# Moving sums of a pooling branch at earlier weight pieces, and two chunks of its products side by side through ScalarE and VectorE

## The chip, the cores and the metric

The kernel runs on one core of a Trainium2 chip. The time is device microseconds (us) of that core for one launch of the whole program: from the inputs in device memory to the output there. The engines of the core are named as the profile names them: PE is TensorE (PEld its weight loads), DVE is VectorE, ACT is ScalarE, POOL is GpSimd, and SP is SyncE, which issues most of the DMA transfers.

## The reference

A trunk of two layers works on 256 tokens of 1024 channels, in float32. Each layer has a token mixer and a gated MLP with a short convolution. The change lies in the mixer's pooling branch. Its part of the reference, with what stands around it (dilated attention, gates and the MLP are left out):

```
D_MODEL, SEQ, DEPTH = 1024, 256, 2
POOL_WINDOWS = (2, 4, 8, 16)
...
def _centred_mean(u, window):
    c = jnp.pad(jnp.cumsum(u.astype(jnp.float32), axis=1), ((0, 0), (1, 0), (0, 0)))
    i = np.arange(S)
    lo = np.clip(i - window // 2, 0, S)
    hi = np.clip(i - window // 2 + window, 0, S)
    count = (hi - lo).astype(np.float32)
    return ((c[:, hi] - c[:, lo]) / count[None, :, None]).astype(u.dtype)
...
def _token_mixer(xn, w_in, w_pool, pool_scale, w_a, w_b, w_o, rel_bias):
    u, q, k, v, g_pool, g_attn = jnp.split(xn @ w_in, SPLITS, axis=-1)
    ug = u.reshape(B, S, POOL_GROUPS, POOL_GROUP_DIM)
    pooled = jnp.stack([_centred_mean(ug[:, :, gi], w) for gi, w in enumerate(POOL_WINDOWS)], axis=2) - ug
    pool_out = jnp.einsum('bsgc,gcd->bsgd', pooled, w_pool).reshape(B, S, POOL_WIDTH) * pool_scale
    ...
    merged = jax.nn.sigmoid(g_pool) * (pool_out @ w_a) + jax.nn.sigmoid(g_attn) * (attn_out @ w_b)
    return merged @ w_o
```

So four groups of 256 channels are each averaged over a centred window of 2, 4, 8 or 16 tokens, the token itself is taken away, each group is multiplied with its own 256 x 256 matrix and scaled per channel, and the result (8 chunks of 128 channels) goes into the product with w_a.

## The kernel before, in words

**Products in two parts.** Every float32 operand of a large product is split into a high part in a reduced format and the rest (a low part), and three products are made: high by high, high by low, low by high. A weight reaches the core as `raw` by DMA from SyncE's queue, ScalarE casts it to the high part `wh` (L214) and VectorE subtracts to get the low part `wl` (L216). The class `Weights` does this in the order of use. A *piece* is 128 x 1024 elements; a load brings two pieces; three raw buffers and five pairs of `wh`, `wl` turn. `W.get()` hands out the next piece, and first writes the splits up to four pieces further on into the program; so a split stands in ScalarE's and VectorE's queues where the piece some four ahead of it is taken. A raw buffer is free for the next load when the low part of its second piece is made.

**Where the branch lies.** In each layer the values come first, then the 1024 channels of u (8 pieces), then query and key rows of the attention: six blocks `n` of 4 pieces each (`by_tokens`, L702, tile `t_ps`). Behind each of these pieces stands a *place*, 0 to 23 for these blocks, and the table `steps` says what is written into the program at which place. From here to the gates the three engines PE, ACT and DVE run in order of the source (`manual_schedule`): an engine never takes a later instruction ahead of one that waits. After a block, its rows are transposed by VectorE (`cross`, L749, tile `qk_rows`), written to device memory by SyncE (`crossing`) and read back by GpSimd's queue.

**The moving sums.** `pool_window(gi)` is a generator for window 2, 4, 8, 16 (`gi` 0 to 3). ScalarE copies u into a padded tile (L1013); VectorE doubles the window by one addition after the other (L1022: one addition for window 2, four for window 16), mends the edges (L1031, L1035), and makes the centred input `pd` (L1037); ScalarE casts its high part (L1045) and VectorE makes its low part `pl` (L1046). It yields after each addition, after `pd`, and after `pl`: 3 + 4 + 5 + 6 = 18 parts for the four windows. `pool(n)` in `steps` runs the next n parts. Before, two parts stand at places 4 to 6, one at 7, two at each of 8 to 12, and one at 13.

**The branch's products.** `pool_out` runs beside block n = 3, whose four pieces are numbered 33, 34, 36 and 37 in layer 0; two more pieces, 32 and 35, hold the four groups' matrices. Ahead of each of the four pieces, one group's products are made (`two_sums`, L578, tile `pool_ps`): two chunks `oc` of 128 channels, eight matmuls each. `pool_ps` takes a buffer of a PSUM pool of four. A chunk then goes through four operations that alternate between two engines: ScalarE multiplies the second half-sum by the scale (L1070), VectorE multiplies the first and adds (L1071, tile `po`; this frees the PSUM buffer), ScalarE casts the high part (L1074), VectorE makes the low part (L1075). The `po` tile turns in three buffers. All four operations of a chunk are written before those of the next.

In the instruction orders below, the numbers behind a tile's name are the program's own; for weights, `wh37` and `wl37` are the two parts of piece 37.

Of the kernel before, what the change touches and what calls it, by code (L numbers as in the profile page):

```python
# [10 lines left out]
F32 = mybir.dt.float32  # L11
F32R = mybir.dt.float32r
AF = mybir.ActivationFunctionType
ALU = mybir.AluOpType
# [240 lines left out]
def encoder(ctx, tc, x, w_in, w_pool, pool_scale, w_a, w_b, w_o, norm1, norm2, w_up, conv_w,  # L255
            conv_b, w_down, rel_bias, norm_f, onehot, edges, out):
    nc = tc.nc
# [43 lines left out]
    for l in range(DEPTH):  # L301
# [11 lines left out]
        for n, pairs in enumerate(BLOCKS):  # L313
            for base in (C_Q, C_K):
                pool = ([], [])
                if n == 1 and base == C_K:
                    pool = W.add(
                        w_pool[l].rearrange("g (k p) c -> p (g k) c", p=P), (8, 256),
                        [((lambda t, j=j: t[:, 4 * j : 4 * j + 4, :]), (4, 256)) for j in range(2)],
                    )  # L320
                    pool = (pool[:1], pool[1:])
# [18 lines left out]
        for kind, n in PLAN:  # L340
            if kind in "AG":
                j = halves_done.get((kind, n), 0)
# [65 lines left out]
    hps = const.tile([P, DEPTH, 8], F32, name="hps")  # L408
# [156 lines left out]
    def two_sums(x2, nk, *chunks):  # L565

        wide, rests = ([(c, k, kind) for c in chunks for k in range(nk)] for kind in (True, False))
        first = rests if turns["rest"] else wide
        last = wide if turns["rest"] else rests
        for steps in (first, last):
            for (ps, wh, wl), k, kind in steps:
                out, w, x = (ps, wh, x2[:, k]) if kind else (ps[:, 1], wl, x2[:, k, 0])
                nc.tensor.matmul(  # L578
                    out, w(k), x, start=(steps is first and k == 0),
                    stop=(steps is last and k == nk - 1), skip_group_check=turns["rest"],  # L580
                )
        turns["rest"] = not turns["rest"]
# [21 lines left out]
    def halves(a):  # L604

        return a.rearrange("p (t m) -> p t m", t=2)
# [86 lines left out]
    def v_tile():  # L693
        return acc.tile([P, 512], F32, tag="acc", name="v_ps")
# [12 lines left out]
    def by_tokens(x2, n, at_once=1, then=None, ps=None, begin=0, end=None,  # L707
                  ahead=None):


        if ps is None:
            ps = [mmp.tile([P, 512], F32, tag="mm", name="t_ps") for _ in range(2)]
        for i0 in range(begin, n if end is None else end, at_once):
            if ahead:
                next(ahead)
            held = [W.get() for _ in range(at_once)]
            for t in range(2):
                for i, piece in enumerate(held, i0):
                    v_sum(ps[t], x2, t, i, piece, n - 1)
            for i, _ in held:  # L720
                W.free(i)
            if then:
                then()
        return ps

    def to_chunks(rows, y, z, parts):

        turned = nc.vector.transpose(out=y.rearrange("p q c j -> p c q j"), in_=rows)  # L730
        d = dram.tile([P, 4, P], F32, tag="turned", bufs=4, name="turned")
        nc.sync.dma_start(out=d, in_=y.rearrange("p q c j -> p q (c j)"))
        for q in range(4):
            there = nc.sync.dma_start(
                out=z[32 * q : 32 * q + 32].rearrange("p a c j -> p a (c j)"),
                in_=d[:, q].rearrange("(a i) x -> i a x", a=4),
            )
        hi, lo = (p.rearrange("p c (a j) -> p a c j", a=4) for p in parts)
        made = nc.scalar.copy(out=hi, in_=z), nc.vector.tensor_sub(out=lo, in0=z, in1=hi.bitcast(F32))
        return turned, there, made  # L740
# [23 lines left out]
    def two_parts(tag, name):  # L764


        return big.tile([P, KD, 2, 2, P], F32R, tag=tag, name=name)
# [174 lines left out]
    for l in range(DEPTH):  # L942
# [25 lines left out]
        else:  # L968
            for g in range(NG):
                held = begun[0] if g == 0 else [W.get() for _ in range(4)]  # L970
                for t in range(2):
                    if g + t == 0:
                        ps = begun[1]
                    else:
                        ps = v_tile()
# [22 lines left out]
        for n in range(2):  # L998
            ps = by_tokens(x2, 4)
# [56 lines left out]
        def pool_out(po2):  # L1056
            for j in range(2):
                i, (wh, wl) = W.get()
                for gg in range(2):
                    for oc in range(2):  # L1060
                        ps = acc.tile([P, 2, S], F32, tag="acc", name="pool_ps")
                        cc = slice(oc * P, (oc + 1) * P)
                        two_sums(
                            pooled[2 * j + gg], 2,
                            (ps, lambda k: wh[:, 2 * gg + k, cc], lambda k: wl[:, 2 * gg + k, cc]),
                        )
                        c = 4 * j + 2 * gg + oc
                        sc = hps[:, l, c : c + 1]
                        po = sm.tile([P, 2, P], F32, tag="p", bufs=3, name="po")
                        nc.scalar.mul(out=po, in_=halves(ps[:, 1]), mul=sc)  # L1070
                        nc.vector.scalar_tensor_tensor(  # L1071
                            out=po, in0=halves(ps[:, 0]), scalar=sc, in1=po, op0=ALU.mult, op1=ALU.add
                        )
                        nc.scalar.copy(out=po2[:, c, 0], in_=po)  # L1074
                        nc.vector.tensor_sub(out=po2[:, c, 1], in0=po, in1=po2[:, c, 0].bitcast(F32))  # L1075
                    if gg:
                        W.free(i)
                    yield
# [103 lines left out]
        def keep_pa(n):  # L1182
# [7 lines left out]

            **{n: ((pool, 2),) for n in (4, 5, 6)},
            7: ((pool, 1),),
            **{n: ((pool, 2),) for n in range(8, 13)},
            13: ((pool, 1),),
            16: ((parts, 0),),
            17: ((parts, 1),),
            19: ((bring, 0),),
# [25 lines left out]
        po2 = None  # L1223
        for n in range(6):
            block, which = divmod(n, 2)
            if n == 3:
                po2 = two_parts("m2", "po2")
            ps = by_tokens(x2, 4, then=step, ahead=pool_out(po2) if n == 3 else None)
            y = rows_of_tmp(1)
            if n in (2, 4):  # L1230
                z = tmp[:, 0].rearrange("p (a c j) -> p a c j", a=8, c=4)
            else:

                z = zu[:, 0] if n == 1 else kk[:, (1, None, None, 0, None, 1)[n]]
            cross(ps, y, z, "crossing")
            if n == 3:

                highs = big.tile([P, 2, HPG, 2, P], F32R, tag="xn", name="highs")
                qh, kh = highs[:, 0], highs[:, 1]
                lows = [  # L1240
                    big.tile([P, 2, 2, 2, P], F32R, tag=f"{tag}0", name="lows") for tag in "qk"
                ]
                turned_p = big.tile([P, 2, 2 * 4, 4, 32], F32, tag="ybig", name="turned_p")
# [15 lines left out]
        for n in range(2):  # L1259
            th = gate("q1")  # L1260
            for t in range(2):
                nc.vector.scalar_tensor_tensor(
                    out=pa[n][:, t], in0=th[:, t], scalar=1.0, in1=pa[n][:, t],
                    op0=ALU.add, op1=ALU.mult,
# [4 lines left out]
        made = None  # L1269
        turned_rows = big.tile([P, 2, 2, 4, 4, 32], F32, tag="xn", name="turned")  # L1270
        for n, cc in enumerate(HALVES):
# [6 lines left out]
            ps = by_tokens(at2, 2, 2)  # L1278
# [3 lines left out]
            for t in range(2):  # L1282

                with tc.issue_after((turning if t else made[1]).ins) if n + t else ExitStack():
                    nc.vector.scalar_tensor_tensor(
                        out=th[:, t], in0=th[:, t], scalar=1.0, in1=ps[t], op0=ALU.add, op1=ALU.mult
                    )
                    nc.vector.tensor_add(out=th[:, t], in0=th[:, t], in1=pa[n][:, t])
                turning, there, made = to_chunks(
                    th[:, t], y[:, t], z[:, t], (mh[:, ks, t], ml[:, ks, t])  # L1290
                )
# [179 lines left out]
```

## Time and profile before

| | |
|---|---|
| median of 3 runs | 862.19 us |
| the runs | 860.63, 862.19, 864.61 us |
| the profiled execution | 862.41 us, of which the profile's span is 860.6 us |
| mean granted TensorE clock | 0.996 |
| PE busy | 848.0 us (99%) |
| DVE, ACT busy | 664.5 us (77%), 489.5 us (57%) |
| pool_ps matmuls | 32 + 32, from 95.5 to 535.0 us (two layers) |

The span runs from the first to the last instruction; the execution's own time is some 2 us longer. Rows of the timeline read: start in us, length in us, engine, source line, operation, output <- inputs, shape, count, and in brackets how long the engine stood idle just before and what released it. Rows of a count over one merge equal instructions, and their length runs from the first start to the last end. Matmuls overlap in these rows, so the pace of PE is read from start to start. Rows of the windows view give for each engine the busy time and the count in that stretch, then the granted TensorE clock, the busy share of the DMA engines and GB/s. SPq and POOLq are the queues that issue DMA.

### The profile page before, as it was taken

The page shows a single profiled execution, that of the slowest core. Times are in us where ns is not written, and L with a number is a line of the kernel's source. Part 1 is how long each engine was busy: PE and PEld are TensorE (multiplying, and loading weights), DVE is VectorE, ACT ScalarE, POOL GpSimd, SP SyncE. Part 2 cuts the span into 40 slices and gives each one's busy share as a digit, 9 for nine tenths or more (in the row PEclk, how much of TensorE's full clock was granted, in tenths as well). Part 3 has the DMA queues.
Part 4 walks back from the last instruction along what each step waited for, and adds up shares of the span by engine and source line. Part 5 has one row for each costly group of instructions (what it writes and reads, how often), then busy time and mean ns, then how long its engine had stood idle before and what let it go on. Part 6 is the DMA issues. An engine that isn't in the chain of part 4 may idle for free.

```text
span 860.6 us, 11236 instructions
## 1 busy us (share of the span) xinstructions
PE 848.0 (99%) x3959; PEld 708.6 (82%) x3959; DVE 664.5 (77%) x994; ACT 489.5 (57%) x759; POOL 133.3 (15%) x274
## 2 busy tenths in 40 slices
PE   9999999999999999999999999999999999999996
PEld 7888878888888888888888887888888888888885
DVE  7957887877767869889855598787676778797894
ACT  7735473655545556667645355655454555666682
POOL 1811212120011221220000212132100122121201
PEclk9999999999999999999999999999999999999999
DMA  9689878994749888976627888788857498798831
GB/s 332 210 245 337 245 244 289 296 310 165 252 176 295 263 274 265 291 264 212 240 98 237 264 257 260 243 274 300 267 187 278 136 304 268 248 294 287 254 143 49
DMA packets 117697, 211.95 MB, mean 246 GB/s; under 512 B 7864, under 2 KB 45440, under 8 KB 117640
## 3 DMA queue, kind: packets, MB, share of 16 engines
q1 hardware_dynamic: 109032, 187.89, 65.5%
q0 software_dynamic: 8448, 23.08, 10.1%
q8 instruction: 31, 0.51, 0.2%
q10 hardware_dynamic: 160, 0.27, 0.1%
q14 instruction: 26, 0.21, 0.1%
HBM read 184.97 MB, written 26.23 MB: 245 GB/s over the span
## 4 chain that ended last, share of the span: by engine, by line
PE 84%; DVE 9%; DMA 3%; issue 1%; ACT 1%; SPq 1%; POOLq 0%; DVEq 0%; POOL 0%; ACTq 0%
PE t_ps L702 51%; PE v_ps L702 6%; PE res_ps L620 6%; PE res_ps L622 5%; PE res_ps L621 5%; DVE wl L216 4%; DMA raw<-in_w_in_dram 3%; PE v_ps L934 3%; PE proj_ps L578 2%; PE v_ps L841 1%; DVE us L1022 1%; PE o_ps L1151 1%; PE s_ps L1098 1%; DVE qk_rows L749 1%; PE s_ps L1092 1%
## 5 line engine op out<-in xcount | busy, mean ns | idle before, releaser
L702 PE MATMUL t_ps<-wh,x 128*128 128x512 f32 x1344 | 421.2, 390 | 0.0
L216 DVE TENSOR_TENSOR wl<-raw,wh 128x1024 fp32r<-128x1024 f32 x274 | 331.0, 1217 | 104.7 <-ACT wh L214 102.0
L214 ACT CAST wh<-raw 128x1024 fp32r<-128x1024 f32 x274 | 285.7, 1050 | 172.9 <-PE t_ps L702 117.0
L702 PEld LDWEIGHTS t_ps<-wh,x 128*128 128x128 f32 x1344 | 252.7, 188 | 52.7
L702 PE MATMUL t_ps<-wl,x 128*128 128x512 f32 x672 | 261.7, 389 | 0.0
L702 PEld LDWEIGHTS t_ps<-wl,x 128*128 128x128 f32 x672 | 126.4, 188 | 25.9
L620 PE MATMUL res_ps<-wh,actq 128*128 128x512 f32 (+1 forms) x184 | 70.2, 381 | 0.1
L621 PE MATMUL res_ps<-wl,actq 128*128 128x512 f32 (+1 forms) x184 | 69.9, 380 | 0.0
L622 PE MATMUL res_ps<-wh,actk 128*128 128x512 f32 (+1 forms) x184 | 69.8, 380 | 0.0
L702 PE MATMUL t_ps<-wh,po 128*128 128x512 f32 x128 | 40.8, 393 | 0.0
L620 PEld LDWEIGHTS res_ps<-wh,actq 128*128 128x128 f32 x184 | 34.6, 188 | 7.5 <-ACT actq L1405 1.0
L622 PEld LDWEIGHTS res_ps<-wh,actk 128*128 128x128 f32 x184 | 34.6, 188 | 6.9 <-DVE actk L1406 0.4
L621 PEld LDWEIGHTS res_ps<-wl,actq 128*128 128x128 f32 x184 | 34.6, 188 | 6.5
L756 POOL DMA_DIRECT2D zga<-crossing x32 | 18.6, 588 | 96.6 <-DMA crossing<-crossing 45.6
L487 POOL TENSOR_SCALAR ss<-ss 128x1 f32<-128x1 f32 x8 | 2.0, 255 | 194.2 <-ACT junk L480 194.2
L756 POOL DMA_DIRECT2D zg<-crossing x32 | 18.4, 583 | 82.5 <-DMA crossing<-crossing 37.4
L1389 ACT ACTIVATE y<-y 128x256 f32<-128x256 f32 x44 | 18.3, 415 | 21.5 <-DVE y L1386 21.1
L756 POOL DMA_DIRECT2D zu<-crossing x24 | 14.2, 596 | 103.6 <-PE t_ps L702 63.0
L1114 ACT ACTIVATE p<-s,nm 128x512 f32<-128x512 f32 x16 | 11.6, 724 | 31.7 <-DVE nm L1111 29.0
L1371 ACT ACTIVATE y<-a,prm 128x256 f32<-128x256 f32 x44 | 26.1, 598 | 5.7 <-DVE y L1390 4.7
L702 PEld LDWEIGHTS t_ps<-wh,po 128*128 128x128 f32 x128 | 24.0, 188 | 4.9
L756 POOL DMA_DIRECT2D turned_p<-turning x32 | 18.6, 590 | 55.9 <-DMA turning<-turning 30.8
(208 smaller groups left out, 1201.2 us busy)
## 6 DMA issues: line engine op xcount, KB each, us to landing
raw<-in_w_up_dram SPq DMA_DIRECT2D x44, 1024.0 KB, 8.3
raw<-in_w_in_dram SPq DMA_DIRECT2D x34, 1024.0 KB, 6.5
raw<-in_w_in_dram SPq DMA_DIRECT2D x50, 512.0 KB, 5.0
raw<-in_w_down_dram SPq DMA_DIRECT2D x22, 1024.0 KB, 7.1
crossing<-crossing SPq DMA_DIRECT2D x20, 512.0 KB, 7.0
crossing<-qk_rows SPq DMA_DIRECT2D x16, 512.0 KB, 6.3
raw<-in_w_a_dram SPq DMA_DIRECT2D x8, 1024.0 KB
raw<-in_w_o_dram SPq DMA_DIRECT2D x8, 1024.0 KB, 4.8
```

The lines of the kernel that those rows point to most:

```text
L214: inst = nc.scalar.copy(out=h, in_=src)
L216: inst = nc.vector.tensor_sub(out=l, in0=src, in1=h.bitcast(F32))
L578: nc.tensor.matmul(out, w(k), x, start=(steps is first and k == 0), stop=(steps is last and k == nk - 1), skip_group_check=turns["rest"],)
L620: nc.tensor.matmul(ps, ah, wh, start=first, stop=False, skip_group_check=on)
L621: nc.tensor.matmul(ps, ah, wl, start=False, stop=False, skip_group_check=on)
L622: nc.tensor.matmul(ps, al, wh, start=False, stop=last, skip_group_check=on)
L702: nc.tensor.matmul(ps, x2[:, 2 * n + j, part, t, :], w[:, j, :], start=(n + m == 0), stop=(n == last and m == 5),)
L756: nc.gpsimd.dma_start(out=z[32 * q : 32 * q + 32].rearrange("p a c j -> p a (c j)"), in_=d[:, q].rearrange("(a i) x -> i a x", i=32),)
L934: nc.tensor.matmul(ps[t], a[:, k, t, :], w[:, j, :], start=(k + m == 0), stop=(k == KD - 1 and m == 2),)
L1114: nc.scalar.activation(p, s, AF.Exp, bias=nm[:, 0:1], accum_out=z)
L1371: nc.scalar.activation(y, a, AF.Identity, bias=b, scale=w1)
L1389: nc.scalar.activation(y2, y2, AF.Tanh, scale=c)
```

## The change

Two things are changed, and both apply to each of the two layers.

First, the table of places. The 18 parts of the moving sums stand at places 4 to 11 in place of 4 to 13: places 4 to 7 keep their parts, then come four, three, three and one in place of two at each of 8 to 12 and one at 13. So all of them are in the program ahead of the transposes of block n = 2 and of the first pool products.

Second, the operations behind the products. For the two chunks of a group, `pool_out` now makes both products first, then both multiplications of ScalarE, both of VectorE, both casts and both subtractions, in place of all four of one chunk and then all four of the other.

```
--- before.py
+++ after.py
@@ -1057,6 +1057,7 @@
             for j in range(2):
                 i, (wh, wl) = W.get()
                 for gg in range(2):
+                    made = []
                     for oc in range(2):
                         ps = acc.tile([P, 2, S], F32, tag="acc", name="pool_ps")
                         cc = slice(oc * P, (oc + 1) * P)
@@ -1064,15 +1065,22 @@
                             pooled[2 * j + gg], 2,
                             (ps, lambda k: wh[:, 2 * gg + k, cc], lambda k: wl[:, 2 * gg + k, cc]),
                         )
-                        c = 4 * j + 2 * gg + oc
-                        sc = hps[:, l, c : c + 1]
                         po = sm.tile([P, 2, P], F32, tag="p", bufs=3, name="po")
-                        nc.scalar.mul(out=po, in_=halves(ps[:, 1]), mul=sc)
+                        made.append((4 * j + 2 * gg + oc, ps, po))
+
+                    for c, ps, po in made:
+                        nc.scalar.mul(out=po, in_=halves(ps[:, 1]), mul=hps[:, l, c : c + 1])
+                    for c, ps, po in made:
                         nc.vector.scalar_tensor_tensor(
-                            out=po, in0=halves(ps[:, 0]), scalar=sc, in1=po, op0=ALU.mult, op1=ALU.add
+                            out=po, in0=halves(ps[:, 0]), scalar=hps[:, l, c : c + 1], in1=po,
+                            op0=ALU.mult, op1=ALU.add,
                         )
+                    for c, _, po in made:
                         nc.scalar.copy(out=po2[:, c, 0], in_=po)
-                        nc.vector.tensor_sub(out=po2[:, c, 1], in0=po, in1=po2[:, c, 0].bitcast(F32))
+                    for c, _, po in made:
+                        nc.vector.tensor_sub(
+                            out=po2[:, c, 1], in0=po, in1=po2[:, c, 0].bitcast(F32)
+                        )
                     if gg:
                         W.free(i)
                     yield
@@ -1190,8 +1198,10 @@
 
             **{n: ((pool, 2),) for n in (4, 5, 6)},
             7: ((pool, 1),),
-            **{n: ((pool, 2),) for n in range(8, 13)},
-            13: ((pool, 1),),
+            8: ((pool, 4),),
+            9: ((pool, 3),),
+            10: ((pool, 3),),
+            11: ((pool, 1),),
             16: ((parts, 0),),
             17: ((parts, 1),),
             19: ((bring, 0),),
```

Two places in the order. VectorE's queue in layer 0, from the last addition of window 16 to the low part of its input, before (`us`, `pd`, `pl2` belong to window 16, `po` and `po2` to the chunks):

```order
L1022 TENSOR_TENSOR us_1046<-us_994 128x2x257
L1031 TENSOR_TENSOR us_1046<-us_1046,edge_81 128x2x8
L1035 TENSOR_TENSOR us_1046<-us_1046,edge_81 128x2x7
L1037 SCALAR_TENSOR_TENSOR pd_1050<-us_1046,u_969 128x512
L1071 SCALAR_TENSOR_TENSOR po_1057<-pool_ps_1052,hps_80,po_1057 128x256
L1075 TENSOR_TENSOR po2_1004<-po_1057,po2_1004 128x256
L1071 SCALAR_TENSOR_TENSOR po_1067<-pool_ps_1062,hps_80,po_1067 128x256
L1075 TENSOR_TENSOR po2_1004<-po_1067,po2_1004 128x256
L216 TENSOR_TENSOR wl37_1073<-raw18_902,wh37_1072 128x1024
L216 TENSOR_TENSOR wl38_1077<-raw19_930,wh38_1076 128x1024
L1046 TENSOR_TENSOR pl2_523<-pd_1050,pl2_523 128x2x256
```

The same queue now, from the last edge product of window 16 to the first four chunk operations:

```order
L1035 TENSOR_TENSOR us_980<-us_980,edge_81 128x2x7
L1037 SCALAR_TENSOR_TENSOR pd_984<-us_980,u_953 128x512
L216 TENSOR_TENSOR wl35_987<-raw16_796,wh35_986 128x1024
L1046 TENSOR_TENSOR pl2_523<-pd_984,pl2_523 128x2x256
L749 STREAM_TRANSPOSE qk_rows_525<-t_ps_896 128x4x4x32
L749 STREAM_TRANSPOSE qk_rows_525<-t_ps_897 128x4x4x32
L216 TENSOR_TENSOR wl36_1016<-raw18_902,wh36_1015 128x1024
L1074 SCALAR_TENSOR_TENSOR po_1027<-pool_ps_1022,hps_80,po_1027 128x256
L1074 SCALAR_TENSOR_TENSOR po_1033<-pool_ps_1028,hps_80,po_1033 128x256
L1081 TENSOR_TENSOR po2_1012<-po_1027,po2_1012 128x256
L1081 TENSOR_TENSOR po2_1012<-po_1033,po2_1012 128x256
```

The low part of window 16 stood behind four chunks and the splits of pieces 37 and 38; now it stands ahead of the transposes, the split of piece 36 and every chunk.

ScalarE's queue in layer 0, where the chunks of windows 8 and 16 stand, before:

```order
L214 CAST wh39_1097<-raw19_930 128x1024
L1070 ACTIVATE po_1106<-pool_ps_1101,hps_80 128x256
L1074 CAST po2_1004<-po_1106 128x256
L1070 ACTIVATE po_1116<-pool_ps_1111,hps_80 128x256
L1074 CAST po2_1004<-po_1116 128x256
```

The same place now:

```order
L214 CAST wh39_1097<-raw19_936 128x1024
L1072 ACTIVATE po_1106<-pool_ps_1101,hps_80 128x256
L1072 ACTIVATE po_1112<-pool_ps_1107,hps_80 128x256
L1079 CAST po2_1012<-po_1106 128x256
L1079 CAST po2_1012<-po_1112 128x256
```

The second chunk's multiplication stands ahead of the first chunk's cast. TensorE's own order is the same before and now, and so are those of SyncE and GpSimd.

## The prediction, made blind

> **What bounds the kernel now.** I read the first part of the page first, then what TensorE waited for, then the order of time around its waits. The page:
>
> ```profile
> span 860.6 us, 11236 instructions
> PE 848.0 (99%) x3959; PEld 708.6 (82%) x3959; DVE 664.5 (77%) x994; ACT 489.5 (57%) x759; POOL 133.3 (15%) x274
> ...
> DMA  9689878994749888976627888788857498798831
> ...
> raw<-in_w_in_dram SPq DMA_DIRECT2D x50, 512.0 KB, 5.0
> ```
>
> (The third row is the DMA engines' busy share in tenths, the last a weight load with its us to landing; both are used further down.) TensorE (PE) is busy for 848.0 of 860.6 us; ahead of its first work and behind its last nobody can fill it. So the change, which leaves TensorE's instructions as they are, can win at most what TensorE idles or loses in between, and can lose whatever new wait it puts there. All that TensorE waited for in the span (total us, times, longest):
>
> ```profile
> PE pool_ps L578 <- DVE pl L1046: 3.8, 2, 1.9
> PE gain_ps L405 <- PEq L1453: 0.8, 1, 0.8
> PE xt_ps L789 <- DMA h<-in_x_dram: 0.7, 1, 0.7
> PE v_ps L841 <- DVE m L232: 0.5, 1, 0.5
> ```
>
> The last three belong to the first 7 us. The first is one stall per layer: the last group of pool products waits for the low part of its input (pl), made by VectorE in L1046. TensorE there, layer 0 and layer 1, with TensorE's granted clock (third value from the end) in three stretches of one us:
>
> ```profile
> 103.77 0.62 PE L578 MATMUL pool_ps<-pl,wh 128*128 128x512 f32 x2
> ...
> 105.17 0.39 PE L702 MATMUL t_ps<-wh,x 128*128 128x512 f32 x1
> ...
> 107.67 0.39 PE L702 MATMUL t_ps<-wh,x 128*128 128x512 f32 x1
> 110.00 0.70 PE L578 MATMUL pool_ps<-pl,wh 128*128 128x512 f32 x2 [1.94 <-DVE pl L1046]
> ...
> 111.48 0.39 PE L702 MATMUL t_ps<-wh,x 128*128 128x512 f32 x1
> ```
>
> ```profile
> 530.61 0.39 PE L702 MATMUL t_ps<-wh,x 128*128 128x512 f32 x1
> 532.82 1.06 PE L578 MATMUL pool_ps<-pl,wh 128*128 128x512 f32 x2 [1.82 <-DVE pl L1046]
> ...
> 535.38 0.63 PE L702 MATMUL t_ps<-wh,x 128*128 128x512 f32 x1
> ...
> 536.76 0.40 PE L702 MATMUL t_ps<-wl,x 128*128 128x512 f32 x1
> ```
>
> ```profile
> 108.00:109.00 1.00, 0.06 (x1) 0.00 (x0) 1.00 (x2) 1.00 (x2) 0.36 (x1) 1.00 0.78 225
> 533.00:534.00 1.00, 1.00 (x4) 0.81 (x4) 1.00 (x2) 0.00 (x0) 0.00 (x0) 0.50 1.05 365
> 536.00:537.00 1.00, 1.00 (x6) 0.77 (x4) 0.86 (x2) 0.45 (x2) 0.00 (x0) 0.81 1.08 381
> ```
>
> In layer 1 the stall costs twice: TensorE stands, and then works on at half its clock until about 536.6. In layer 0 the clock stays at 1.00.
>
> Why pl is late, on VectorE and ScalarE in layer 0:
>
> ```profile
> 87.75 0.72 DVE L1022 TENSOR_TENSOR us<-u 128x542 f32<-128x542 f32 x1
> 88.50 0.72 DVE L1022 TENSOR_TENSOR us<-us 128x538 f32<-128x538 f32 x1
> 89.14 1.22 DVE L216 TENSOR_TENSOR wl<-raw,wh 128x1024 fp32r<-128x1024 f32 x1
> 90.28 0.70 DVE L1022 TENSOR_TENSOR us<-us 128x530 f32<-128x530 f32 x1
> ...
> 91.29 0.69 DVE L1037 SCALAR_TENSOR_TENSOR pd<-us,u 128x512 f32<-128x512 f32 x1
> 91.90 1.22 DVE L216 TENSOR_TENSOR wl<-raw,wh 128x1024 fp32r<-128x1024 f32 x1
> 93.03 0.69 DVE L1046 TENSOR_TENSOR pl<-pd,pl 128x512 fp32r<-128x512 f32 x1
> ...
> 93.88 0.72 DVE L1022 TENSOR_TENSOR us<-u 128x542 f32<-128x542 f32 x1
> ...
> 97.03 1.31 DVE L749 STREAM_TRANSPOSE qk_rows<-t_ps 128x512 f32<-128x512 f32 x2
> 98.26 1.18 DVE L216 TENSOR_TENSOR wl<-raw,wh 128x1024 fp32r<-128x1024 f32 x1
> 99.36 0.47 DVE L1071 SCALAR_TENSOR_TENSOR po<-pool_ps,hps,po 128x256 f32<-128x256 f32 x1
> ...
> 102.04 0.69 DVE L1022 TENSOR_TENSOR us<-us 128x514 f32<-128x514 f32 x1
> ...
> 103.05 0.69 DVE L1037 SCALAR_TENSOR_TENSOR pd<-us,u 128x512 f32<-128x512 f32 x1
> ...
> 105.94 0.42 DVE L1075 TENSOR_TENSOR po<-po,po 128x256 fp32r<-128x256 f32 x1 [0.47 <-ACT po L1074]
> 106.89 2.36 DVE L216 TENSOR_TENSOR wl<-raw,wh 128x1024 fp32r<-128x1024 f32 x2 [0.52 <-ACT wh L214]
> 109.17 0.69 DVE L1046 TENSOR_TENSOR pl<-pd,pl 128x512 fp32r<-128x512 f32 x1
> ```
>
> ```profile
> 105.82 1.99 ACT L214 CAST wh<-raw 128x1024 fp32r<-128x1024 f32 x2
> 107.71 0.65 ACT L1045 CAST pl<-pd 128x512 fp32r<-128x512 f32 x1
> ```
>
> The centred input pd of window 16 is there at 103.74. Its split stands behind four chunks' chains and two weight splits, and ends at 109.86, while TensorE could have begun at 107.67 + 0.23 = 107.90 (a start to the next is about 0.23 us there).
>
> **The change part by part.** *The stalls, removed.* Layer 0: from 107.67 the next start comes after 2.33 us in place of 0.23, so 2.10 us, and the block behind it takes 111.48 - 110.00 = 1.48 us against 105.17 - 103.77 = 1.40, so 0.08 more. Layer 1: 532.82 - 530.61 = 2.21, less 0.23: 1.98; the block 535.38 - 532.82 = 2.56 against 1.40: 1.16; then four matmuls in 1.38 against 4 x 0.23 = 0.92: 0.46. Together 2.18 + 3.60 = 5.8 us, of which 1.62 are the lowered clock.
>
> By the Trainium skill, "TensorE: Matmul & The Clock Gate", section "Part 1: The HAM clock gate", the clock is halved after an idle window of some 3.4 us that runs free of the kernel. By that rule, a gap of 2 us takes no clock, 1.62 us are not the stall's, and the sum would be 4.2 us. The trace differs on the length (0.50 stands right behind a gap of 1.82 us), and agrees that it is a matter of phase (1.00 after 1.94 us). I take the trace.
>
> *Does pl come in time?* VectorE's two orders stand with the change above. Window 16 is finished ahead of the query rows' transposes, not behind four chunks. No instruction is new; the moved ones are the third and fourth sum, two edge products, pd and the split. VectorE has no room at this place, so they push back what they pass: I add starts from the rows above. Window 8's second sum starts at 88.50 as before; third sum 89.25 (a sum 0.75 behind the last); pd 90.26 (+1.01, as 90.28 to 91.29); weight 33's low part 90.87 (+0.61); pl of window 8 92.00 (+1.13); window 16: sums at 92.85 and 93.60, weight 34 at 94.24 (+0.64), sums at 95.38 (+1.14) and 96.13, pd 97.14 (+1.01), weight 35 at 97.75, **pl at 98.88, done at 99.57**; transposes 99.57, weight 36 at 100.80 (+1.23), first chunk 101.90 (+1.10), done at 102.37. ScalarE's part is its cast of pd (0.65), between 97.83 and 98.88. So pl is there 8.3 us ahead of 107.90. Layer 1's order is the same, its rows stand 422.9 us later.
>
> *What is pushed back.* Weight 34 ends 2.3 us later at 95.5 (TensorE wants it about 101.0), weight 35 at 99.0 (wanted 104.2), weight 36 2.5 us later at 102.0 (wanted 105.4). The nearest to the edge is a wait on VectorE that now stands behind more work: the fifth group of products, at 103.77, takes the PSUM buffer of the first, which the first chunk's VectorE operation frees, 99.83 before, 102.37 now. **1.4 us are left**, and 1.5 for the sixth. That is the cover; gone, every us more would be TensorE's, in each layer.
>
> *The loads and the crossing.* SyncE's issues, each waiting for the buffer that a weight split frees:
>
> ```profile
> 93.14 3.54 SPq L151 DMA_DIRECT2D raw<-in_w_in_dram  x4
> ```
>
> These four bring the loads of weights 38 to 41. They go behind weights 34 and 35 now, at 95.5 and 99.0 instead of 93.1 and 95.7. Taking 7 us to land (the page's row has 5.0), the last are there at 106; weight 38 was cast behind 106.8, the second of the casts at 105.82, and TensorE wants it at 112. Behind them on SyncE stands the query rows' crossing, which waits for the transposes, at 101 instead of 98.4, and behind that the issue that waits for weight 37, which comes a little earlier than before (below). GpSimd's copies back of these rows come 2.5 us later, and TensorE uses those rows only at place 24, thirty us on. Nothing of this reaches TensorE.
>
> *The chunks side by side.* ScalarE's order for two chunks, with the change above, was multiply, cast, multiply, cast; it is now two multiplies, two casts. VectorE need no longer idle on each cast for the 0.47 us that the row at 105.94 shows. A pair took 102.04 - 99.36 = 2.68 us; VectorE's own work in it is 2 x 0.48 + 2 x 0.42 = 1.8. Nothing of this alone is on TensorE's path. Its bounds: from 101.90 four chunks end by 105.5 (1.8 a pair) or 107.3 (no gain at all). Weight 37's low part was done 2.2 us behind the start of the last chunk's last operation (105.94 to 108.1), so now at 107.3, or at 109.1. TensorE wants it at 107.90 + 1.40 + 0.23 = 109.53. So even with no gain there is no stall; I take the first, since VectorE is full there, and the price is 0 at both ends.
>
> **Sum.** The profiled execution took 862.41 us, span 860.6; less 5.8 gives **856.6 us**. The median before, 862.19, lies 0.2 below that execution, so the ratio stays 0.993.
>
> **The rivals.** *The half clock is not the stall's*, or it comes at another place: the gain is 5.8 - 1.62 = 4.2 us, the time 862.41 - 4.2 = 858.2. For it: 1.94 us of standing left the clock at 1.00 in layer 0. (The rule of the Trainium skill cited above would have it so.) Against it: in slices of 2 us, from 8 us to the last matmul, there is no other below 1.00. Chance 0.10.
>
> *VectorE is later than my sum and part of the stall returns at the fifth products' PSUM buffer*: 1 us beyond the 1.4 left, in both layers, gives 858.6. For it: the sum has some fifteen links without a gap. Against it: each is a start to start that VectorE kept in these rows. 0.07.
>
> *Given back downstream*: once TensorE is 2 us earlier, a load ends last. For it: the DMA engines stand at 9 tenths in eight slices of the page's row. Against it: not one wait of TensorE on a weight in the whole span, and the split pipeline runs up to four pieces (11 us) ahead. All given back: 862, no change. 0.08.
>
> *Slower*: the same PSUM wait, but VectorE 5 us late (a cast of ScalarE behind a held-up weight buffer, say), so 3.6 us of standing and 1.6 of half clock in both layers, 10.4 on top: 867. It decides from 4.3 us late on (2.9 us in each layer, the gain gone). 0.03.
>
> **How the numbers follow.** The forecast has 0.72. The 0.5% that a measurement of this kernel can tell from no change is 4.3 us, below 857.9. Faster: the forecast's 0.72; same: the three middle rivals, 0.25; slower 0.03. The range runs from 855.2 (runs before spread by 2 us to either side) to 859.0, which takes in the first two rivals and leaves out about 0.15.
>
> **What would show it.** Right: no wait of TensorE on pl or pool_ps, granted clock 1.00 from 8 us on to the last matmul; pl of window 16 near 99.6, the first chunk's VectorE operation near 101.9, the gap from 103.77 to the seventh products 4.1 us. Wrong: a wait of pool_ps on po (L1074), a t_ps wait on wl or wh, or a stretch at 0.50.

## The result, and the profile after

| | before | after |
|---|---|---|
| median of 6 runs each | 862.9 us (860.63 to 864.61) | 857.52 us (857.32 to 858.38) |
| ratio of the medians | | 0.9944, 95% interval 0.9926 to 0.9962 |
| the profiled execution | 862.41 us, span 860.6 | 857.50 us, span 855.7 |

The changed kernel is faster by 0.56%. The first part of its page and all that TensorE waited for in it (us in total, times, longest):

```profile
span 855.7 us, 11232 instructions
PE 848.1 (99%) x3959; PEld 709.5 (83%) x3959; DVE 664.9 (78%) x994; ACT 489.1 (57%) x759; POOL 132.6 (15%) x274
```

```profile
PE gain_ps L405 <- PEq L1463: 0.8, 1, 0.8
```

PE, DVE and ACT are busy as long as before to 0.4 us, and the two waits of `pool_ps` on `pl` are gone; what is left is the program's start. TensorE in order of time around the two places, layer 0 and then layer 1 (start, length, engine, line, operation). Products are counted by chunks: a chunk takes four matmuls, so a group's block has eight, the fifth products are the first chunk of window 8, and the seventh are the first of window 16.

```profile
104.78 0.62 PE L578 MATMUL pool_ps<-pl,wh 128*128 128x512 f32 x2
...
108.68 0.39 PE L702 MATMUL t_ps<-wh,x 128*128 128x512 f32 x1
108.90 0.61 PE L578 MATMUL pool_ps<-pl,wh 128*128 128x512 f32 x2
...
110.30 0.39 PE L702 MATMUL t_ps<-wh,x 128*128 128x512 f32 x1
...
529.34 0.39 PE L702 MATMUL t_ps<-wh,x 128*128 128x512 f32 x1
529.56 0.62 PE L578 MATMUL pool_ps<-pl,wh 128*128 128x512 f32 x2
...
530.96 0.39 PE L702 MATMUL t_ps<-wh,x 128*128 128x512 f32 x1
```

The seventh products follow the matmul ahead of them after 0.22 us in both layers, where it was 2.33 and 2.21, and their block takes 1.40 in both (110.30 - 108.90, 530.96 - 529.56), where it was 1.48 and 2.56. The granted clock is the third value from the end in these stretches of one us:

```profile
108.00:109.00 1.00, 1.00 (x6) 0.84 (x5) 1.00 (x2) 1.00 (x2) 0.00 (x0) 1.00 0.05 10
533.00:534.00 1.00, 1.00 (x6) 0.83 (x5) 0.92 (x4) 0.91 (x3) 0.00 (x0) 1.00 1.10 333
```

TensorE is busy throughout and the clock stays at 1.00, in layer 1 too. VectorE in layer 0:

```profile
99.99 0.68 DVE L1046 TENSOR_TENSOR pl<-pd,pl 128x512 fp32r<-128x512 f32 x1
100.59 1.30 DVE L749 STREAM_TRANSPOSE qk_rows<-t_ps 128x512 f32<-128x512 f32 x2
...
102.92 0.86 DVE L1074 SCALAR_TENSOR_TENSOR po<-pool_ps,hps,po 128x256 f32<-128x256 f32 x2
...
104.64 0.87 DVE L1074 SCALAR_TENSOR_TENSOR po<-pool_ps,hps,po 128x256 f32<-128x256 f32 x2
...
106.94 3.50 DVE L216 TENSOR_TENSOR wl<-raw,wh 128x1024 fp32r<-128x1024 f32 x3 [0.53 <-ACT wh L214]
...
114.37 2.36 DVE L216 TENSOR_TENSOR wl<-raw,wh 128x1024 fp32r<-128x1024 f32 x2 [0.53 <-ACT wh L214]
```

The low part of window 16's input ends at 100.67, ahead of the transposes. A pair of chunks takes 1.72 us (102.92 to 104.64), where it took 2.68.

Laid matmul by matmul beside the trace of before, after gains 2.19 us at the seventh products of layer 0 and 3.61 in layer 1 (1.98 at once, the rest on the matmuls that had run at half clock, 0.2 on each wide one), and 0.07 at one matmul in between. It loses 0.96 in the first 9 us, where the pace of the matmuls doubles later. Together 4.91, and the spans differ by 4.9. These are the first matmuls of the values, before and after:

```profile
7.37 0.94 PE L841 MATMUL v_ps<-m,xuh 128*128 128x512 f32 x3
```

```profile
7.95 1.31 PE L841 MATMUL v_ps<-m,xuh 128*128 128x512 f32 x3
```

The same three take 0.94 us and 1.31. The kernel's order at the start is the same in both; a second profile of after (below) starts like before.

### The profile page after: what moved, and what is told of

It reads as the page before. It is cut to its first block, busy times and chain, and to the rows that moved or that the text cites. A ratio compares the mean times of both kernels' runs of the same rounds, so it can differ in the third digit from the quotient of the medians.

```text
span 855.7 us, 11232 instructions
## 1 busy us (share of the span) xinstructions
PE 848.1 (99%) x3959; PEld 709.5 (83%) x3959; DVE 664.9 (78%) x994; ACT 489.1 (57%) x759; POOL 132.6 (15%) x274
## 4 chain that ended last, share of the span: by engine, by line
PE 96%; DVE 2%; DMA 1%; ACT 0%; issue 0%; POOLq 0%; POOL 0%; DVEq 0%; ACTq 0%
PE t_ps L702 61%; PE v_ps L702 6%; PE res_ps L620 6%; PE res_ps L622 5%; PE res_ps L621 5%; PE v_ps L934 3%; PE proj_ps L578 2%; PE v_ps L841 1%; PE pool_ps L578 1%; DVE wl L216 1%; PE o_ps L1159 1%; PE s_ps L1106 1%; PE s_ps L1100 1%; PE o_ps L1155 1%; PE xt_ps L514 1%; DMA raw<-in_w_in_dram 1%
```

## The experiments

The theory with which I went to the chip: TensorE gains its two stalls and the half clock behind one of them because `pl` comes in time, so the places do it, and the chunks side by side are worth nothing on TensorE's path. Its rivals: the half clock is not the stall's; and the chunks' order is what makes room for the moved sums. In each diff the kernel that it starts from is named. Ratios are against the kernel before on the same chip.

**The places alone** (from before).

```
-            **{n: ((pool, 2),) for n in range(8, 13)},
-            13: ((pool, 1),),
+            8: ((pool, 4),),
+            9: ((pool, 3),),
+            10: ((pool, 3),),
+            11: ((pool, 1),),
```

> The moving sums at places 4 to 11 alone; the chunks one after the other as before. Theory (the late low part of window 16 is the whole stall; the chunks' order is off TensorE's path): no wait of TensorE on pl, the time of the changed kernel, 857.5 us within 0.5. The nearest wait is weight 37's low part: with 2.68 us a pair it is done 0.5 us ahead of TensorE's wish. Rival (the side by side chunks are needed, because the sums now crowd VectorE ahead of them): TensorE waits on wl (L216) or wh at piece 37 in both layers, 858.5 us or more.

Measured: 860.96 us (858.39 to 863.41, 12 runs), ratio 0.9973 [0.9959, 0.9986]. That is half of the gain, and not the 857.5 expected. What TensorE waited for:

```profile
PE t_ps L702 <- DVE wl L216: 1.0, 2, 0.6
...
PE o_ps L1147 <- DVE ptl L1138: 0.3, 1, 0.3
...
PE s_ps L1098 <- DMA k<-crossing: 0.2, 1, 0.2
```

`pl` is in time, as forecast: no wait on it is left. These waits stand behind it instead. In order of time, TensorE and then VectorE:

```profile
107.98 0.62 PE L578 MATMUL pool_ps<-pl,wh 128*128 128x512 f32 x2
...
118.52 0.50 PE L702 MATMUL t_ps<-wl,x 128*128 128x512 f32 x1 [0.58 <-DVE wl L216]
...
165.22 0.39 PE L1147 MATMUL o_ps<-ptl,vh 128*128 128x256 f32 x1 [0.34 <-DVE ptl L1138]
```

```profile
107.92 3.50 DVE L216 TENSOR_TENSOR wl<-raw,wh 128x1024 fp32r<-128x1024 f32 x3 [0.53 <-ACT wh L214]
...
117.24 2.36 DVE L216 TENSOR_TENSOR wl<-raw,wh 128x1024 fp32r<-128x1024 f32 x2 [0.53 <-ACT wh L214]
```

The last row begins with the low part of weight 40. It starts 117.24 - 107.98 = 9.26 us behind the seventh products; in after 114.37 - 108.90 = 5.47. VectorE is 3.79 us later there, and TensorE waits. At weight 37 (the row that begins at 107.92) it was 1.90 later by the same reckoning, and nothing waited. Laid matmul by matmul beside the trace of after, this one loses 0.85 us at weight 40 in layer 0 and 0.68 in layer 1, and 0.95, 0.26 and 0.42 in the attention; with smaller steps, 3.5 in all behind the first 15 us. In the kernel before, the same low part starts here:

```profile
116.80 2.36 DVE L216 TENSOR_TENSOR wl<-raw,wh 128x1024 fp32r<-128x1024 f32 x2 [0.53 <-ACT wh L214]
```

That is 116.80 - 110.00 = 6.80 us behind its seventh products, 2.46 less than with the places alone: TensorE stood for 2 us ahead of them, and VectorE worked on. The chain of waits that ends at the `o_ps` row shows how lateness reaches the attention:

```profile
129.00 10.33 DMA crossing<-qk_rows
...
147.32 7.46 DMA turning<-turning
...
155.35 1.72 POOL turned_p L756 x3
157.07 6.66 DMA turned_p<-turning
...
164.48 0.70 DVE ptl L1138
```

The probabilities' way out to memory and back is issued at 147.32 (144.45 in after) and GpSimd's copies back at 155.35 (147.94), each behind a transfer of 7 us and more. Of the 7.4 us by which the copies are later, 2.9 are the issue's; the way out itself took 7.46 us here, where in after the copies began 3.49 us behind the issue. Why this transfer was the longer one is left open. In after the page's chain of waits is TensorE's to 96%, here to 75%. So a rival holds: moved sums push VectorE back, and something has to give the time back.

**Side by side alone** (from after, with the places of before).

```
-            8: ((pool, 4),),
-            9: ((pool, 3),),
-            10: ((pool, 3),),
-            11: ((pool, 1),),
+            **{n: ((pool, 2),) for n in range(8, 13)},
+            13: ((pool, 1),),
```

> The chunks side by side alone; the moving sums at places 4 to 13 as before. Theory (a stall is as long as pl is late, whatever makes it late): two pairs of chunks stand ahead of pl and each gets about 0.95 us shorter (2.68 to 1.72), so pl ends 1.9 us earlier, at 107.9 in the clock of the kernel before, and TensorE still waits about 0.2 us in each layer: 857.9 us, between 857.3 and 858.6, without a stretch of half clock. Rival (the places make the gain, the side by side chunks nothing): the time of the kernel before, 862 to 863 us.

Measured: 858.87 us (857.79 to 859.59, 5 runs), ratio 0.9948 [0.9933, 0.9963].

```profile
PE pool_ps L578 <- DVE pl L1046: 0.5, 1, 0.5
```

The part that I had priced at nothing brings most of the gain alone, since `pl` stands behind the chunks here and they end sooner. 0.50 us are left of the stall in layer 0 and 0.1 in layer 1. Places alone take 0.27% off, chunks alone 0.52%, both 0.56%: the two don't add up, as both go at the same stall.

**The last part one place later** (from before): does a stall cost its full length?

```
-            13: ((pool, 1),),
+            14: ((pool, 1),),
```

> The kernel before, with the last part of the moving sums (the split of window 16's input) one place later, at 14 in place of 13: one weight split and two more chunks stand ahead of it on VectorE. Theory (a stall of TensorE there is paid in full, and a half clock on top when it is long): pl ends at about 113.7 in the clock of the kernel before, TensorE stands 5.9 us in each layer in place of 2.1, and the clock falls in both: 857.5 + 2 x 5.9 + 2 x 1.6 = 872.5 us, between 871 and 874. Rival (part of a stall is made up later, where splits and loads have caught up): under 869 us.

Measured: 874.12 us (872.41 to 875.07, 4 runs), ratio 1.0125 [1.0107, 1.0144].

```profile
PE pool_ps L578 <- DVE pl L1046: 11.7, 2, 5.9
```

The stalls are 5.87 and 5.79 us, 3.9 to 4.0 more than before, and are paid in full. The profiled execution took 872.41: 862.41 + 2 x 4.0 = 870.4, and the rest is a half clock that now comes in both layers, and for two stretches of 3.41 us in each. The granted clock in layer 0, in stretches of 3.41 us:

```profile
106.77:110.18 3.41, 1.26 (x6) 0.72 (x4) 3.36 (x3) 2.28 (x4) 1.27 (x3) 1.00 0.70 188
110.18:113.60 3.42, 0.00 (x0) 0.00 (x0) 2.35 (x6) 1.74 (x4) 0.00 (x0) 0.50 1.03 342
113.60:117.01 3.41, 3.11 (x9) 2.67 (x10) 0.64 (x2) 0.84 (x3) 0.00 (x0) 0.50 0.70 238
```

The clock fell at 110.18, behind a stretch in which TensorE had worked 1.26 of 3.41 us, and stayed down through the next two. So nothing behind the stall catches the loss up. The median lies 0.1 above the expected 871 to 874.

**Is the cover 1.4 us?** (from after). The centred input of window 16 is made five times in place of once, ahead of the first chunk.

```
-            nc.vector.scalar_tensor_tensor(
...
+            for _ in range(5 if gi == 3 else 1):
+                nc.vector.scalar_tensor_tensor(
...
```

> The changed kernel, with the operation that makes window 16's centred input done five times in place of once (same result): four more operations of 0.61 to 0.75 us, 2.4 to 3.0 us, on VectorE ahead of everything that the change pushed back. Theory (1.4 us are left at the PSUM buffer of the fifth products): TensorE waits for po (the chunk operation of VectorE) 1.0 to 1.6 us in each layer, 857.5 + 2.0 to 3.2 = 859.5 to 860.7 us, plus 1.6 for each layer whose clock falls. Rival (the cover is larger, or the wait is another): no wait there, 857.5 us, or a wait on weights 36 or 37.

Measured: 860.82 us (859.55 to 861.7, 10 runs), ratio 0.997 [0.996, 0.9981].

```profile
PE pool_ps L578 <- DVE po L1075: 2.9, 2, 1.6
```

```profile
99.21 3.60 DVE L1038 SCALAR_TENSOR_TENSOR pd<-us,u 128x512 f32<-128x512 f32 x5
```

```profile
105.78:109.19 3.41, 1.86 (x10) 1.65 (x11) 3.28 (x7) 1.64 (x5) 0.00 (x0) 1.00 1.06 381
109.19:112.60 3.41, 3.41 (x19) 2.89 (x18) 2.80 (x5) 3.41 (x6) 1.70 (x3) 1.00 0.26 87
```

(L1075 is the chunk operation in this kernel.) The five operations took 3.60 us where the one took 0.69, so 2.9 more. The wait stands at the fifth products' PSUM buffer, where the prediction had put the edge: TensorE idled 1.65 us in layer 0 and 1.26 in layer 1, and lost 1.92 and 1.53 beside the trace of after. That leaves a cover of 1.0 to 1.4 us (2.9 - 1.92, 2.9 - 1.53). The time is 0.1 above the expected 859.5 to 860.7. The clock did not fall behind 1.55 us of standing (3.41 - 1.86).

**After again**, with a new profile on another chip.

> The changed kernel once more, beside the next three on the same chip: 857.5 us within 1, no wait of TensorE on pl, po, wl or wh, no stretch of half clock before the last matmul.

Measured: 858.23 us (856.44 to 858.33, 6 runs), ratio 0.9941 [0.9925, 0.9956]. The profiled execution is the one of 856.44; it has no wait behind its first 7 us and runs at the full pace from 3.7 us on, 1.06 us ahead of the first profile of after (857.50). Against the profiled 862.41 of before, which starts in the same way, the gain is 5.97 us.

**A stall between** (from before). The centred input of window 16 made three times: does the clock fall behind 3.3 us of standing, or only behind a whole idle stretch of 3.4?

```
+            for _ in range(3 if gi == 3 else 1):
                 nc.vector.scalar_tensor_tensor(
                     out=pd, in0=cur[:, :, o : o + S], scalar=1.0 / w, in1=u[:, :, PAD : PAD + S],
...
```

> The kernel before, with the operation that makes window 16's centred input done three times in place of once (same result), so that pl is later by two operations of 0.61 to 0.75 us. Theory (the stall is paid in full, and the clock falls at the end of a 3.41 us stretch in which TensorE idled more than about half): stalls of 3.2 to 3.4 us in both layers in place of 1.94 and 1.82, each falling over more than 1.7 us of one stretch in nearly every execution, so two falls in place of none to two: 857.5 + 2 x 3.4 + 2 x 1.7 = 867.7 us, between 866 and 869, mean clock 0.995 or lower in every run. Rival (a fall needs a whole idle stretch of 3.4 us): no fall, 864 to 865 us, clock as in the changed kernel.

Measured: 868.65 us (868.07 to 870.33, 4 runs), ratio 1.0063 [1.0041, 1.0084].

```profile
PE pool_ps L578 <- DVE pl L1047: 6.7, 2, 3.4
```

```profile
108.34:111.76 3.42, 1.07 (x5) 0.56 (x3) 2.44 (x3) 3.40 (x5) 0.52 (x1) 1.00 0.42 121
111.76:115.17 3.41, 2.32 (x8) 2.06 (x9) 2.94 (x6) 1.55 (x4) 0.00 (x0) 0.50 0.92 292
535.01:538.42 3.41, 1.45 (x7) 0.87 (x5) 2.41 (x4) 3.19 (x5) 1.32 (x3) 1.00 0.55 154
538.42:541.84 3.42, 2.11 (x7) 1.95 (x8) 2.95 (x5) 1.68 (x4) 0.00 (x0) 0.50 0.83 267
```

The clock fell in both layers, behind 2.35 and 1.96 us of standing in a stretch of 3.41. It stayed down for a second stretch where TensorE had stood for 1.1 and 1.3 us of the first (3.41 - 2.32, 3.42 - 2.11). The rival that asks for a whole idle stretch falls. The Trainium skill, "TensorE: Matmul & The Clock Gate", section "Part 1: The HAM clock gate", has the clock halved after an idle window of about 3.4 us: no stretch here was idle as a whole, so the measurement decides against that length; that the windows run free of the kernel agrees with these traces.

**Is half of the chunks' gain enough?** If all that counts is whether VectorE is in time at weight 40, half of the 3.8 us should remove the waits; if each us of lateness costs its share, half of the loss should stay. The chunks of windows 2 and 4 are side by side here, those of windows 8 and 16 go one after the other (from after).

```
+                    for batch in [made] if j == 0 else [made[:1], made[1:]]:
-                    for c, ps, po in made:
+                        for c, ps, po in batch:
...
```

> The changed kernel, with the chunks of windows 2 and 4 side by side and those of windows 8 and 16 one after the other. With all chunks one after the other the splits behind them came 3.8 us later, and weight 40's low part 0.8 us too late. Theory A (a margin: what counts is whether VectorE is in time): half of that, 1.9 us, is won back, weight 40 comes in time, and the time is the changed kernel's within 0.7 us, 857.5 to 858.2 us. Theory B (every us that VectorE is late comes out as a share of time): half way between the two, 859 us and more, with waits on wl or in the attention.

Measured: 856.55 us (856.33 to 858.46, 6 runs), ratio 0.9931 [0.9914, 0.9947]. No wait but those of the start and one of 0.2 us on `res_ps`. Half of the chunks' gain is enough: weight 40's low part starts 2.5 us later than in after in layer 0 and 1.9 in layer 1, and TensorE does not wait for it. Its interval overlaps that of after on the same chip, so it is not shown to be the faster of the two.

**VectorE late at weight 40 alone** (from after). The last low parts are made six times: ten operations more, 3.4 us on VectorE, behind window 16's chunks.

```
-                    for c, _, po in made:
+                    for c, _, po in made * (6 if j and gg else 1):
```

> The changed kernel, with the last two low parts of the chunks made six times in place of once (same result), ten operations of about 0.39 us on VectorE behind the last pair of chunks and ahead of weight 40's low part: 3.9 us in each layer, with ScalarE's and the chunks' order as in the changed kernel. Theory (what the chunks one after the other cost is VectorE's lateness behind them and no more): waits on wl at piece 40 of 0.5 to 1.0 us in both layers, and later ones in the attention through transfers that are issued later: 860 to 861.5 us. Rival (the order of the chunks counts by another way, ScalarE's casts or PSUM): 857.5 to 858.5 us.

Measured: 857.74 us (856.66 to 860.53, 6 runs), ratio 0.9943 [0.9925, 0.9962]; a smaller loss than the expected 860 to 861.5, and within the rival's range. TensorE and VectorE:

```profile
107.99 0.61 PE L578 MATMUL pool_ps<-pl,wh 128*128 128x512 f32 x2
...
118.16 0.50 PE L702 MATMUL t_ps<-wl,x 128*128 128x512 f32 x1 [0.22 <-DVE wl L216]
```

```profile
116.90 2.35 DVE L216 TENSOR_TENSOR wl<-raw,wh 128x1024 fp32r<-128x1024 f32 x2
```

Weight 40's low part starts 8.91 us behind the seventh products, 3.44 later than in after. TensorE loses 0.49 us there in layer 0 and another 0.32 in its attention; in layer 1 VectorE is only 2.75 us later and nothing is lost. With the 3.79 us and 0.85 of the places alone, this puts after's room at weight 40 at about 3 us (3.44 - 0.49, 3.79 - 0.85). I had taken it for smaller.

**Late at both weights** (from after): six operations more behind window 4's chunks, five behind window 16's.

```
-                    for c, _, po in made:
+                    more = (made * 3, made * 2 + made[:1])[j] if gg else []
+                    for c, _, po in made + more:
```

> The changed kernel, chunks side by side, with low parts of chunks made again (same result) where the chunks one after the other lost VectorE's time: six more operations of 0.35 us behind window 4's chunks, ahead of weights 37 to 39, and five behind window 16's, ahead of weight 40. VectorE is then 2.1 us later at weight 37 and 3.8 us at weight 40, as with the chunks one after the other (1.9 and 3.8), but ScalarE's order is the changed kernel's. Theory (VectorE's lateness at both places, and the loads issued behind it, make what the chunks one after the other cost): waits on weight 40's low part of 0.7 to 0.9 us in both layers and waits in the attention, 860 to 861.5 us. Rival (with 3.4 us late at weight 40 alone the cost was 0 to 1 us, so the rest comes from ScalarE's order, not from VectorE's time): 857.5 to 859 us.

Measured: 858.32 us (856.65 to 858.69, 5 runs), ratio 0.9946 [0.9931, 0.996].

```profile
PE s_ps L1107 <- DMA k<-crossing: 1.0, 1, 1.0
```

VectorE was only 2.29 us later at weight 40, inside the room of 3, and nothing waited there; one wait of 1.0 us stood in layer 1's attention. The dose was too small to answer the question.

**The right dose** (from after), and the places alone again on the same chip: eight and seven operations more.

```
-                    for c, _, po in made:
+                    more = (made * 4, made * 3 + made[:1])[j] if gg else []
+                    for c, _, po in made + more:
```

> As the run before it with low parts of chunks made again, but eight and seven operations more in place of six and five, since those made VectorE only 1.2 us late at weight 37 and 2.3 us at weight 40 (0.5 us of idle time took some of it up). Now 1.9 and about 3.7 us, as with the chunks one after the other. TensorE's margin at weight 40 is 3.0 us by the runs so far (3.44 late: a wait of 0.43; 3.79 late: 0.82; 2.29 late: none). Theory (VectorE's lateness is all that the chunks one after the other cost): waits on weight 40 of 0.6 to 0.9 us in both layers, further waits in the attention, a median of 860 us or more, as the next run has it. Rival (ScalarE's order adds to it): waits on weight 40, but a median of 859.3 us or less, over 1 us below the next run.

> The moving sums at places 4 to 11 alone once more, on the same chip as the run before: 860 to 861.5 us, with waits on weight 40's low part of 0.6 to 0.9 us in both layers and waits in the attention that differ from execution to execution.

Measured: 862.15 us (858.46 to 863.74, 11 runs), ratio 0.998 [0.9968, 0.9993], and for the places alone 861.91 (858.23 to 865.31, 10 runs), ratio 0.9973 [0.9956, 0.999]. First the kernel with the dose, TensorE and VectorE:

```profile
108.87 0.61 PE L578 MATMUL pool_ps<-pl,wh 128*128 128x512 f32 x2
...
119.26 0.50 PE L702 MATMUL t_ps<-wl,x 128*128 128x512 f32 x1 [0.44 <-DVE wl L216]
```

```profile
117.98 2.36 DVE L216 TENSOR_TENSOR wl<-raw,wh 128x1024 fp32r<-128x1024 f32 x2
```

and TensorE's waits on low parts of weights with the places alone, the second time:

```profile
PE t_ps L702 <- DVE wl L216: 2.2, 3, 1.2
```

With its chunks side by side but VectorE 117.98 - 108.87 - 5.47 = 3.64 us late at weight 40, the changed kernel takes as long as the places alone, and not the 859.3 or less that another effect of the order would have left. So the chunks' order matters by the time that it saves on VectorE, and this lateness is what took much of the places' gain; with runs that spread over 5 and 7 us, a further effect of an us or two could not be told. How much the single waits cost differs from execution to execution, as this row against the first time's 1.0 shows; which transfer of the attention is late in which run was not settled.

## Why the prediction came out right, and where it did not

- **The time.** 856.6 was forecast, within 855.2 to 859.0, and 857.52 was measured: faster by 0.56%, with an interval of 0.38 to 0.74%.
- **The stalls.** Forecast 2.10 + 0.08 us in layer 0 and 1.98 + 1.16 + 0.46 in layer 1; measured 2.19 and 3.61, together 5.8 as forecast. Half clock and stall go together, so the rival in which the half clock is not the stall's falls, with the runs at longer stalls (868.65 and 874.12) and with after, where neither is left. Which layer pays for it seems a matter of phase, not of the kernel: eleven runs of before had a mean clock of 0.999, too high for a fall (3.41 us at half clock take 0.002 off the mean), and took 860.66 to 862.45; they have no trace.
- **What the sum left out.** The start: 0.96 us against the profiled execution, and the whole miss of 0.9. Against the execution of after that starts like before's, the gain was 5.97, forecast 5.8.
- **`pl` in time.** Forecast done at 99.57, measured 99.7 (100.67 less the 1.0 of the start); first chunk operation forecast at 101.90, measured 101.9; room at the fifth products forecast 1.4, measured 1.39; from the fifth to the seventh products forecast 4.1, measured 108.90 - 104.78 = 4.12. The chain of some fifteen links held to about 0.1 us, and 2.9 us more on it cost 1.92 and 1.53 at exactly that place. The rival at this buffer and the slower one did not come about.
- **The step that failed: the chunks side by side, "Nothing of this alone is on TensorE's path", price 0 at both ends.** The bound was worked out for the first four of a layer's eight chunks and checked at weight 37, and there it holds: without the gain VectorE is 1.90 us later and nothing waits. The other four chunks stand between weight 37 and weight 40. A pair saves 2.68 - 1.72 = 0.96 us, four pairs 3.84; measured at weight 40: 3.79. The room there is about 3, so without the gain TensorE loses 0.85 and 0.68 there in the two layers, and more in the attention. The price of that step is 0.9973 - 0.9944, or 2.5 us, by the ratios, and 3.5 by the two traces. It did not fall due, because the change makes the chunks faster: the sum was right by the part that it had put at nothing, and that is luck. In the kernel before, the chunks were on TensorE's path as well: two pairs stand ahead of `pl`, and side by side they alone took 0.52% off.
- **"Given back downstream"** (chance 0.08, 862 us) is thus in part what the places do by themselves: 860.96 and 861.91, ratio 0.9973 both times, so about half was given back, not all. The mechanism was not a load that ends last, but VectorE's split of weight 40 and, behind it, the attention's transfers. Until the stall was gone, VectorE caught up in the 2 us in which TensorE stood: the split came 6.80 us behind the seventh products, and without the 2.19 it would have been 8.99 (an estimate from these two), past the 8.4 from which TensorE waits (9.26 - 0.85, 8.91 - 0.49).

## What to carry to other kernels

A stall of the engine that bounds is also the time in which the engines behind it catch up. Whoever removes it by moving their work forward should follow each of them past the stall to the next three or four places where the bounding engine takes something from them, and write the room at each; here it was 1.4 us at the PSUM buffer and 3 at weight 40. Two chains that alternate between two engines are worth laying side by side even where no wait shows it: that was 0.96 us of VectorE for each pair here, at no instruction more.

## What the runs showed of the hardware that was not expected

**The clock's grid.** The granted clock changes only at instants 3.413 us apart, in all these traces: before was at 1.00 for 529.07 us, at 0.50 for 3.41 and at 1.00 for 320.85, which is 155, 1 and 94 times that, and in the runs without a fall inside the work the stretch at 1.00 measured 247 to 250 times. Laid on this grid, the two stalls of before read:

```profile
106.30:109.71 3.41, 1.76 (x8) 1.13 (x6) 2.89 (x4) 3.38 (x5) 2.06 (x4) 1.00 0.54 148
109.71:113.12 3.41, 3.12 (x16) 2.69 (x17) 2.53 (x5) 1.15 (x4) 0.00 (x0) 1.00 1.01 323
529.55:532.96 3.41, 1.59 (x8) 1.04 (x7) 3.25 (x4) 2.96 (x5) 1.23 (x3) 1.00 0.73 199
532.96:536.38 3.42, 3.42 (x11) 2.84 (x12) 2.48 (x6) 1.56 (x4) 0.00 (x0) 0.50 1.05 360
```

Layer 0's stall of 1.94 us lay across an instant of the grid: 1.65 us idle in one stretch, 0.29 in the next, and the clock stayed. Layer 1's 1.82 lay in one stretch, and the next ran at 0.50. Around the stalls of all these runs it stayed behind 1.55 and 1.65 us idle and fell behind 1.82, 1.96, 2.15, 2.35 and a whole stretch. It also stayed behind 1.76 us at the end of the matmuls in the run with the chunks alone (848.68 to 852.09). So the bound lies between 1.76 and 1.82 by the profile's ends of matmuls, a little over half of a stretch. A stall of 1.8 to 1.9 us cost another 1.6 us here or nothing, by phase.

**The start.** By the pace of the matmuls the clock went up at 3.9 us in the profiled execution of before, at 3.7 and 8.8 in the two of after, and at 10.2 in the one with the longer cover. Laid matmul by matmul beside each other, these starts differ by up to 1.7 us. The runs of after and of the version with half of the chunks side by side lie in two groups, at 856.3 to 857.5 and at 858.2 to 858.5; the three profiled ones are all in the first, so that the start makes the groups is not shown. A profile's own time should be set beside its kernel's other runs before a difference of one us is read from it.
